# Gated DeltaNet: another order of the input products in the first two stretches, and other slots for the recurrences and inversions

## The chip, the cores and the metric

The kernel runs on one core of a Trainium2 chip. The metric is the device time of one execution, in microseconds (us). The engines of the core are PE (matrix products; its weight loads are counted apart as PEld), DVE (vector arithmetic), ACT (scalar functions and copies), POOL (a second, slower vector engine) and SP, which only issues DMAs here.

## The reference, cut to what matters

One inference step of a two-layer decoder trunk runs over 1104 tokens: a prompt of 1024, 16 meta tokens ahead of it and 64 tokens of eight sampled sequences. Layer 0 is a Gated DeltaNet with 8 key heads and 16 value heads of 128; layer 1 is an RWKV-7 layer that the change does not touch. Of layer 0:

```python
qkv, z, b, a = split(xn @ w_in)                 # 1024 -> 2*1024 + 2048 + 2048 + 32
qkv = silu(causal_conv(qkv, width 4))
q, k = l2norm(q), l2norm(k);  beta = sigmoid(b);  g = -exp(a_log) * softplus(a + dt_bias)
# per value head, chunk by chunk:
A = eye + strict_lower((k*beta) @ k.T * decay)
u, wk = solve(A, [v*beta, k*beta*exp(gc)])      # unit lower triangular
attn = lower(q @ k.T * decay)
v_new = u - wk @ S
o = (q*exp(gc)) @ S + attn @ v_new
S = S*exp(g_last) + k_dec.T @ v_new             # the recurrence over chunks
out = rmsnorm(o) * silu(z) @ w_out
```

The triangular solve needs the inverse of A for each chunk of 128 tokens, and S is carried from chunk to chunk.

## The kernel before

Layer 0 runs over eight **pairs** j = 0 to 7, one key head and its two value heads each. The input projection is done feature tile by feature tile of 128: keys k, queries q, the values v and w of the two heads, and the gates z and z' of the two heads (products x and y in the changed kernel). Each such product goes over three token segments of 384, 384 and 336, and each segment in two halves of 12 matmuls (an fp32 product as sums over high and low parts, `xc`, `xa`, `whi`, `wlo`). A half is called a **slot** here; a product is six slots. `products` in `layer0` yields them: 24 slots for k q v w of pair 0, numbered -24 to -1, and then 36 in each **stretch**: k of pair j, z z' of pair j-1, q, v, w of pair j. The last 12 are the gates of pair 7.

All the other work of the layer hangs on these slots. `gdn_events` fills a table of functions by a slot number, a fraction allowed, with `at(u, f)`; ahead of each slot, `before(u)` runs the functions that are due. PE and ACT then work in exactly the order in which the program writes their instructions. DVE, POOL and SP do not: a scheduler with its own idea of how long things take orders their instructions at compile time. What it chose is read from the order of the instructions. Each engine then works through its own list in order, and an instruction that waits holds up all behind it.

`front_events(j, ...)` prepares pair j, once its keys are there:
- decays, exponentials and the scores of k with k for the three segments (events `ed`, `ee`, `es`), which give A;
- the inversion of the diagonal 32x32 blocks of A, all 72 of them side by side (`inverse32`). It has 31 steps, and each is two DVE instructions: a product into `invtmp` (L570) and a subtraction from `invT` (L572), of growing and then shrinking shapes, from 72x31 to 72x256 and back to 72x31. The events `inv` issue them, two steps at a time (three for pair 0);
- `spread` (event `sp`): what is left of the steps, a turned copy (L740), the write of both to DRAM (g_t L743, g_u L742), and the reads back in another layout into `T1n` (L746) and `TT` (L753), all issued on SP;
- four merges, which build the inverse of 128 from blocks of 32: y32, u32, y64, u64, at 6.5, 4.5, 3.5 and 1.5 before a. y32 is the first that reads `T1n`; on PE it writes `rY`, and its DVE copies are L764;
- loads and products of the eight samples' states.

`chain_events(j, ..., a)` is the recurrence of pair j, from slot a = `first[j]` on: nine groups of tokens, each over three slots, for both heads. On DVE a group has X (L880, value rows less what the state gives), S (L902, the new state) and o (L913, the output); on PE these are the `rA` products. In group n, X comes at a + 3n - 1, S and o at a + 3n + 1. The recurrence of pair j-1 is thus running while the blocks of pair j are inverted, and DVE does both, with the conv taps (`cvy`, L523, four to a segment), the value rows (`vt`, `bv`) and the gate rows (`zg`).

Of the kernel before, what the change touches and what calls it, by code (L numbers as in the profile page):

```python
# [22 lines left out]
NEG = -1.0e30  # L23
ZF = 1
QF = 0


class Ctx:
# [7 lines left out]
class Builder:  # L36
# [883 lines left out]
    def gdn_events(self, G, open_, gate, swap):  # L920

        self.events = {}
        base = [36 * (j - 1) for j in range(9)]
        first = [9, 43] + [base[j + 1] + 6 for j in range(2, 8)]
        for u in (-22.9, -19.4, -16.8, -16.7, -16.6):
            self.at(u, gate)
        self.at(-13, swap)
        for j in range(8):
            self.chain_events(j, G, first[j])
            if j:  # L930
                self.front_events(j, G, base[j], base[j] + 18, first[j], open_, base[j] + max(0.3, first[j - 1] - base[j] - 3.4))
            else:
                self.front_events(0, G, -24, -18, first[0], None, None)

    def at(self, u, f, *a):
        self.events.setdefault(u, []).append(lambda: f(*a))
# [55 lines left out]
            for h in (0, 1):  # L992
                at((14.5, 23.5, 30.5)[s] + h, lambda s=s, h=h: self.gdn_norm_out(j, G[j], s, h))

    def front_events(self, j, G, b, qb, a, open_, e):

        g, at = lambda: G[j], self.at
        Sb = {}

        def states(h, q):  # L1000
            Sb[h, q] = self.sample_states(j, h, q)

        def read(h):
            self.gdn_sample_read(g(), h, [Sb[h, q] for q in (0, 1)])
        va = qb + 6
        at(b + 0.1, lambda: self.gdn_prep(j, g()))
        if j:
            at(b - 5.7, open_, j)
            at(b - 1.4, lambda: self.history_turn(g().H))
            k = max(b + 5.5, e + 4.7)  # L1010
            ed, ee, es = [e + 2 * s for s in range(3)], [k + 2 * s - 1.8 for s in range(3)], [k + 2 * s for s in range(3)]
            inv, per, kk, ss, rd = [k + 9.3 + n for n in range(15)], 2, (b + 11.8, qb + 4.2), b + 13.2, (qb + 6.4, qb + 9.9)
            sp = a - 9.9
        else:
            ed, ee, es = [-18.5, -18.4, -18.3], [-16, -15.2, -14.4], [-15.2, -14.4, -13.6]
            inv, per, kk, ss, rd = [-11.5 + n for n in range(10)], 3, (-12.2, -12.1), -12.8, (-7.6, -4.1)
            sp = -1
        for s in range(3):
            at(ed[s], lambda s=s: g().decay(s))
            for tt in range(3):  # L1020
                at(ee[s] + (0.7 if j else 0.25) * tt, lambda s=s, tt=tt: g().exps(s, tt))
            at(es[s], lambda s=s: g().scores(s))
            at(qb + (7.6, 16.4, 20.4)[s], lambda s=s: self.gdn_query_norms(g(), s))
        at(es[2] + 0.4, lambda: g().scales())
        at(es[2] + 0.7, lambda: g().blocks())
        for u in inv:
            at(u, lambda: g().steps(per))
        at(sp, lambda: g().spread())
        for n, u in enumerate((-6.5, -4.5, -3.5, -1.5)):
            at(a + u, lambda n=n: g().merges[n]())  # L1030
        at(kk[0], lambda: self.gdn_sample_keys(g(), 0))
        at(kk[1], lambda: self.gdn_sample_keys(g(), 1))
        for h, q in ((0, 0), (0, 1), (1, 0)):
            at(ss, states, h, q)
        at(rd[0], read, 0)
        at(rd[0] + 0.1, states, 1, 1)
        at(rd[1], read, 1)
        for h in (0, 1):
            for s in range(3):
                at(va + 6 * h + 5.4 + 2 * s, lambda h=h, s=s: self.gdn_value_rows(g(), h, s))  # L1040
        at(va + 12.95, lambda: self.last_tokens(j, g().H))

    def gdn_norm(self, j, G, s, os, ssq):

# [1077 lines left out]
    def layer0(self, top, right, xa, xc):  # L2122
# [20 lines left out]
        kh, kl = [h[:, k] for h in hi for k in range(4)], [l[:, k] for h in lo for l in h for k in range(l.shape[1])]  # L2143
# [3 lines left out]
        G = [None] * 8  # L2147
# [11 lines left out]
        self.gdn_events(G, open_, lambda: next(gate, None), swap)  # L2159

        def products():
            yield from G[0].keys(0)
            yield from self.gdn_queries(0, G[0], kh, kl, 2048)
            yield from self.gdn_values(0, G[0], 0, kh, kl, 2176)
            yield from self.gdn_values(0, G[0], 1, kh, kl, 1152)
            for j in range(1, 8):
                k = 128 * (j + 1)
                z = [4096 + 256 * (j - 1), 4224 + 256 * (j - 1)]
                va = 2048 + 256 * j
                yield from G[j].keys(z[0])  # L2170
                yield from self.gdn_gate(j - 1, G[j - 1], 0, kh, kl, z[1])
                yield from self.gdn_gate(j - 1, G[j - 1], 1, kh, kl, 128 * j)
                yield from self.gdn_queries(j, G[j], kh, kl, va)
                yield from self.gdn_values(j, G[j], 0, kh, kl, va + 128)
                yield from self.gdn_values(j, G[j], 1, kh, kl, 1024 + k if j < 7 else 4096 + 256 * 7)
            yield from self.gdn_gate(7, G[7], 0, kh, kl, 4224 + 256 * 7)
            yield from self.gdn_gate(7, G[7], 1, kh, kl)

        def before(u):
            while True:  # L2180
# [6 lines left out]
        with tc.manual_schedule(engines={mybir.EngineType.PE, mybir.EngineType.Activation}):  # L2187
            self.slot = -24
            for _ in products():
                before(self.slot + 1)  # L2190
                self.slot += 1
# [6 lines left out]
        sp = pool("stage", stage, side="right")  # L2198
# [343 lines left out]
```

## Time and profile before

| what | us |
|---|---|
| median of three runs | 2201.82 |
| lowest and highest | 2195.72, 2205.32 |
| the profiled execution | 2193.46 |
| its span, first to last instruction | 2191.7 |
| PE busy | 2051.0 (94%) |
| DVE busy | 1588.0 (72%) |
| ACT busy | 1291.8 (59%) |
| stretch 1, slots 0 to 35 | 141.9 |
| stretch 2 | 136.1 |
| stretch 3 | 119.2 |
| stretch 4 | 119.5 |

All times in the trace count from the start of the span. The shares of the whole span are means over two layers and many stretches; what the change does is read from the stretches. A row of a timeline is: start, duration, engine, line, operation, output and inputs, shapes, count, and in brackets the idle time of the engine ahead of it and what ended that. A row of waits is: the engine and line that waited, what it waited for, sum, times, longest. A row of windows is: from and to, length, then for each engine its busy time and, in brackets, its instructions, and at the end the granted PE clock (1.00 is full speed), the busy share of the DMA engines and GB/s. A row of groups is: line, engine, operation, names, shapes, count, busy time in us and mean of one in ns, and the idle time ahead of them.

### The profile page before, as it was taken

The page shows a single profiled execution, that of the slowest core. Times are in us where ns is not written, and L with a number is a line of the kernel's source. Part 1 is how long each engine was busy: PE and PEld are TensorE (multiplying, and loading weights), DVE is VectorE, ACT ScalarE, POOL GpSimd, SP SyncE. Part 2 cuts the span into 40 slices and gives each one's busy share as a digit, 9 for nine tenths or more (in the row PEclk, how much of TensorE's full clock was granted, in tenths as well). Part 3 has the DMA queues.
Part 4 walks back from the last instruction along what each step waited for, and adds up shares of the span by engine and source line. Part 5 has one row for each costly group of instructions (what it writes and reads, how often), then busy time and mean ns, then how long its engine had stood idle before and what let it go on. Part 6 is the DMA issues. An engine that isn't in the chain of part 4 may idle for free. (4 is left out here: it accounts for less than half of the span.)

```text
span 2191.7 us, 54812 instructions
## 1 busy us (share of the span) xinstructions
PE 2051.0 (94%) x20404; PEld 1908.7 (87%) x20404; DVE 1588.0 (72%) x4221; ACT 1291.8 (59%) x3761; POOL 844.7 (39%) x1125
## 2 busy tenths in 40 slices
PE   6869899999999999999899999889999999999997
PEld 5859799899999999999899999889888988888876
DVE  7967869788887979695334676757969657767755
ACT  5526466656566565656633365664847446777774
POOL 3423333334333333334231362344534344444444
PEclk9979999999999999999999999899999999999998
DMA  4423342333333433335345215655555376677764
GB/s 118 119 58 90 86 111 78 102 90 97 104 105 97 112 83 103 110 98 145 121 125 128 67 53 190 211 168 173 171 168 163 115 222 174 180 229 226 234 178 136
DMA packets 430661, 292.64 MB, mean 134 GB/s; under 512 B 147146, under 2 KB 412987, under 8 KB 430395
## 3 DMA queue, kind: packets, MB, share of 16 engines
q1 hardware_dynamic: 430394, 289.14, 45.9%
q8 instruction: 161, 2.64, 0.5%
q14 instruction: 106, 0.86, 0.1%
HBM read 197.68 MB, written 91.37 MB: 132 GB/s over the span
## 5 line engine op out<-in xcount | busy, mean ns | idle before, releaser
L90 POOL TENSOR_TENSOR wlo<-wraw,whi 128x512 fp32r<-128x512 f32 (+1 forms) x246 | 330.6, 1346 | 469.5 <-ACT whi L86 434.9
L76 PE MATMUL d<-xc,whi 128*128 128x384 f32 (+2 forms) x1006 | 279.7, 336 | 4.6 <-ACT whi L86 3.9
L523 DVE SCALAR_TENSOR_TENSOR cvy<-raw,cw,cvy 128x408 f32<-128x408 f32 (+2 forms) x288 | 192.5, 669 | 20.3 <-ACT cvy L62 18.8
L86 ACT CAST whi<-wraw 128x512 fp32r<-128x512 f32 (+1 forms) x246 | 149.7, 611 | 86.4 <-PE d L76 48.8
L76 PEld LDWEIGHTS d<-xc,whi 128*128 128x128 f32 (+1 forms) x1006 | 183.2, 189 | 7.4 <-ACT whi L86 4.6
L76 PE MATMUL d<-xc,wlo 128*128 128x384 f32 (+3 forms) x476 | 157.4, 339 | 2.6 <-POOL wlo L90 2.6
L76 PE MATMUL dz<-xc,whi 128*128 128x384 f32 (+1 forms) x480 | 153.7, 338 | 0.0
L76 PE MATMUL dv<-xc,whi 128*128 128x384 f32 (+1 forms) x480 | 152.2, 337 | 0.0
L76 PE MATMUL d<-xa,whi 128*128 128x384 f32 (+3 forms) x450 | 143.2, 342 | 1.6 <-DVE xb L1160 1.2
L62 ACT ACTIVATE o<-rA,gcol 128x128 f32<-128x128 f32 x128 | 42.1, 366 | 117.6 <-DVE S L902 117.3
L570 DVE TENSOR_TENSOR invtmp<-invA,invT 72x31 f32<-72x31 f32 (+15 forms) x248 | 102.5, 413 | 3.2
L76 PE MATMUL dv<-xa,whi 128*128 128x384 f32 (+1 forms) x288 | 99.0, 344 | 0.0
L572 DVE TENSOR_TENSOR invT<-invT,invtmp 72x31 f32<-72x31 f32 (+15 forms) x248 | 96.1, 388 | 3.3
L76 PE MATMUL dz<-xa,whi 128*128 128x384 f32 (+1 forms) x288 | 98.5, 342 | 0.0
L76 PEld LDWEIGHTS d<-xc,wlo 128*128 128x128 f32 (+1 forms) x476 | 89.2, 189 | 6.3 <-POOL wlo L90 3.5
L76 PEld LDWEIGHTS dz<-xc,whi 128*128 128x128 f32 x480 | 89.3, 188 | 4.6 <-issue 4.6
L76 PEld LDWEIGHTS dv<-xc,whi 128*128 128x128 f32 x480 | 89.1, 188 | 1.4 <-issue 1.4
L76 PEld LDWEIGHTS d<-xa,whi 128*128 128x128 f32 (+1 forms) x450 | 85.2, 192 | 4.8 <-issue 3.3
L76 PE MATMUL d<-xa,wlo 128*128 128x384 f32 (+3 forms) x252 | 85.6, 340 | 1.4 <-POOL wlo L90 1.4
L76 PE MATMUL dq<-xc,whi 128*128 128x384 f32 (+1 forms) x240 | 78.0, 342 | 3.0 <-ACT whi L86 3.0
L76 PE MATMUL dk<-xc,whi 128*128 128x384 f32 (+1 forms) x240 | 78.6, 347 | 0.0
L62 ACT ACTIVATE mixs<-xb,omu 128x64 f32<-128x64 f32 (+3 forms) x128 | 61.6, 521 | 18.3 <-DVE xc L90 8.6
(523 smaller groups left out, 6829.5 us busy)
## 6 DMA issues: line engine op xcount, KB each, us to landing
wraw<-in_gdn_w_in SPq DMA_DIRECT2D x96, 256.0 KB
wraw<-in_rwkv_w_rkvz SPq DMA_DIRECT2D x80, 256.0 KB
Sb<-in_state_gdn SPq DMA_DIRECT2D x64, 256.0 KB
sldcak<-cakd SPq DMA_DIRECT2D x24, 576.0 KB
wraw<-in_rwkv_w_o SPq DMA_DIRECT2D x42, 256.0 KB
E<-drow SPq DMA_DIRECT2D x24, 384.0 KB
attn<-drow SPq DMA_DIRECT2D x24, 384.0 KB
wraw<-in_gdn_w_out SPq DMA_DIRECT2D x36, 256.0 KB
```

Of the source, the lines that this page charges most:

```text
L62: return self.nc.scalar.activation(out, in_, func, bias=bias, scale=scale, **kw)
L76: self.nc.tensor.matmul(out, lhsT, rhs, start=start, stop=stop)
L86: nc.scalar.copy(hi, x)
L90: e.tensor_tensor(lo, x, hi.bitcast(F32), op=ALU.subtract)
L523: nc.vector.scalar_tensor_tensor(y[0][:, 0:wd], raw[:, k:k + wd], cw[k], y[0][:, 0:wd], op0=ALU.mult, op1=ALU.add)
L570: nc.vector.tensor_tensor(tmp, A[:, j, j + 1:32].unsqueeze(2).broadcast_to([nb, n, m]), Tv[:, j, 0:m].unsqueeze(1).broadcast_to([nb, n, m] ...
L572: nc.vector.tensor_tensor(Tv[:, j + 1:32, 0:m], Tv[:, j + 1:32, 0:m], tmp, op=ALU.subtract)
```

## The change

The order of the products stands in a table, `ORDER`, one string for each stretch. Stretch 1 has the gates of pair 0 first, then k v q w; stretch 2 has v ahead of q; stretch 3 on are as before. The slots `first`, at which the recurrences start, go from 9, 43, 78, 114 to 11, 47, 80, 114 for pairs 0 to 3, so that a merge of the same pair moves with them; pairs 4 to 7 keep theirs. The times of the other events are tied to the slot of the product that they need and to the start `a0` of the recurrence of the pair before. With k later in stretch 1, pair 1's scores start 7.2 slots later; its inversion events go from 19.6 to 33.6 to 26.2 to 38.1, its spread from 33.1 to 39.25. Pair 2's scores are 4 slots later, its spread 1.95. The inversion events of all pairs but 0 come every 0.85 slots instead of every slot, and for pairs 4 to 7 their spread is 3 slots earlier, and the loads of the samples' states 3.9 slots earlier. What is computed, and each instruction's kind and shape, stay as they are.

```diff
+ORDER = ("kqvw", "xykvqw", "kxyvqw", "kxyqvw", "kxyqvw", "kxyqvw", "kxyqvw", "kxyqvwXY")
...
-        first = [9, 43] + [base[j + 1] + 6 for j in range(2, 8)]
+        first = [11, 47, 80, 114] + [base[j + 1] + 6 for j in range(4, 8)]
...
-            if j:
-                self.front_events(j, G, base[j], base[j] + 18, first[j], open_, base[j] + max(0.3, first[j - 1] - base[j] - 3.4))
-            else:
-                self.front_events(0, G, -24, -18, first[0], None, None)
+            self.front_events(j, G, base[j] if j else -24, first[j], first[j - 1] if j else None, open_)
...
-    def front_events(self, j, G, b, qb, a, open_, e):
+    def front_events(self, j, G, b, a, a0, open_):
...
-        va = qb + 6
+        kb, qb, va, vb = (b + 6 * ORDER[j].index(c) for c in "kqvw")
...
-            k = max(b + 5.5, e + 4.7)
+            e = max(kb + 0.3, a0 - 3.4)
+            k = max(kb + 5.5, e + 4.7)
...
-            inv, per, kk, ss, rd = [k + 9.3 + n for n in range(15)], 2, (b + 11.8, qb + 4.2), b + 13.2, (qb + 6.4, qb + 9.9)
-            sp = a - 9.9
+            inv, per = [k + 8.7 + 0.85 * n for n in range(15)], 2
+            sp = max(k + 9 + 15 * 0.85, a0 + 17.2)
+            ss = max(kb + 6, a0 + 3.3)
+            kk = max(kb + 5.3, b + 11.8), qb + 4.2
+            u = max(qb + 6.4, a0 + 9.5)
+            rd = u, u + 3.5
...
-        for h in (0, 1):
-            for s in range(3):
-                at(va + 6 * h + 5.4 + 2 * s, lambda h=h, s=s: self.gdn_value_rows(g(), h, s))
-        at(va + 12.95, lambda: self.last_tokens(j, g().H))
+        for s in range(3):
+            for h, v in ((0, va), (1, vb)):
+                u = max(v + 5.4 + 2 * s, a0 + 9 * s + 5.8 + 0.2 * h if j else -99)
+                at(u, lambda h=h, s=s: self.gdn_value_rows(g(), h, s))
+        at(vb + 6.95, lambda: self.last_tokens(j, g().H))
```

`products` now walks through `ORDER` and calls the same functions as before, each with the weights of the product that follows it.

Three places show how the instructions move. A number behind a name is a tile's count in its program, and differs between the two kernels. The first place is PE around y32 of pair 0 (`rY`), at the start of stretch 1; `dk` and `dz` are halves of a key and a gate product. Before:

```order
L76 MATMUL dk_1479<-xa_103,whi_1267 128x384
L76 MATMUL dk_1479<-xa_103,wlo_1268 128x384
L76 MATMUL dk_1479<-xc_107,whi_1267 128x384
L73 MATMUL fss_1496<-ident_74,Q_1014 128x128 x3
L76 MATMUL rY_1504<-T1n_513,E_666 32x32 x12
L76 MATMUL rY_1505<-T1n_513,E_678 32x32 x12
L76 MATMUL rY_1506<-T1n_513,E_686 32x32 x12
L76 MATMUL dk_1479<-xc_107,whi_1332 128x384
```

and now:

```order
L77 MATMUL dz_1513<-xa_103,whi_1267 128x336
L77 MATMUL dz_1513<-xa_103,wlo_1268 128x336
L77 MATMUL dz_1513<-xc_107,whi_1267 128x336
L77 MATMUL rY_1530<-T1n_513,E_666 32x32 x12
L77 MATMUL rY_1531<-T1n_513,E_678 32x32 x12
L77 MATMUL rY_1532<-T1n_513,E_686 32x32 x12
L77 MATMUL dz_1513<-xc_107,whi_1332 128x336
```

The merge stood in the second segment of a key product and stands now in the third of a gate product, two slots on.

The second place is DVE where the inversion of pair 1 begins (the first `invtmp` row of 72x31), with the recurrence of pair 0 around it. Before:

```order
L880 SCALAR_TENSOR_TENSOR X_2236<-rA_2240,gcol_123,bv_1209 128x128
L880 SCALAR_TENSOR_TENSOR X_2237<-rA_2241,gcol_123,bv_1209 128x128
L1047 SCALAR_TENSOR_TENSOR ovar_2257<-ssq_1818,qeps_1005 128x6
L110 TENSOR_TENSOR on_t_2260<-ors_2259 128x6
L111 SCALAR_TENSOR_TENSOR on_t_2260<-on_t_2260,ovar_2257 128x6
L112 SCALAR_TENSOR_TENSOR ors_2259<-on_t_2260,ors_2259 128x6
L902 SCALAR_TENSOR_TENSOR S_1817<-S_1817,eglb_124,rA_2240 128x128
L902 SCALAR_TENSOR_TENSOR S_1817<-S_1817,eglb_124,rA_2241 128x128
L570 TENSOR_TENSOR invtmp_2328<-invA_2175,invT_2177 72x31
L572 TENSOR_TENSOR invT_2177<-invT_2177,invtmp_2328 72x31
L913 TENSOR_TENSOR o_2235<-o_2235,rA_2240 128x128
```

and now:

```order
L903 SCALAR_TENSOR_TENSOR S_1801<-S_1801,eglb_124,rA_2387 128x128
L524 SCALAR_TENSOR_TENSOR cvy_2441<-raw_2358,cw_393,cvy_2441 128x336
L914 TENSOR_TENSOR o_2381<-o_2381,rA_2386 128x128
L914 TENSOR_TENSOR o_2381<-o_2381,rA_2387 128x128
L524 SCALAR_TENSOR_TENSOR cvy_2441<-raw_2358,cw_393,cvy_2441 128x336
L881 SCALAR_TENSOR_TENSOR X_2500<-rA_2504,gcol_123,bv_1209 128x128
L881 SCALAR_TENSOR_TENSOR X_2501<-rA_2505,gcol_123,bv_1209 128x128
L571 TENSOR_TENSOR invtmp_2557<-invA_2396,invT_2398 72x31
L1069 SCALAR_TENSOR_TENSOR zg_1444<-mog_2522,hgn_402,zg_1444 128x384
L573 TENSOR_TENSOR invT_2398<-invT_2398,invtmp_2557 72x31
```

The first step stood behind S of group 3 of pair 0; it stands now behind X of group 5.

The third place is DVE where the inversion of pair 5 begins, in a later stretch. Before:

```order
L880 SCALAR_TENSOR_TENSOR X_9078<-rA_9082,gcol_123,bv_8116 128x128
L831 SCALAR_TENSOR_TENSOR zg_9122<-zg_9122,dz_9062 128x384
L110 TENSOR_TENSOR on_t_9105<-ors_9104 128x6
L111 SCALAR_TENSOR_TENSOR on_t_9105<-on_t_9105,ovar_9102 128x6
L112 SCALAR_TENSOR_TENSOR ors_9104<-on_t_9105,ors_9104 128x6
L902 SCALAR_TENSOR_TENSOR S_8651<-S_8651,eglb_124,rA_9081 128x128
L902 SCALAR_TENSOR_TENSOR S_8651<-S_8651,eglb_124,rA_9082 128x128
L570 TENSOR_TENSOR invtmp_9165<-invA_8993,invT_8995 72x31
```

and now:

```order
L881 SCALAR_TENSOR_TENSOR X_9078<-rA_9082,gcol_123,bv_8139 128x128
L571 TENSOR_TENSOR invtmp_9129<-invA_8999,invT_9001 72x31
L573 TENSOR_TENSOR invT_9001<-invT_9001,invtmp_9129 72x31
L571 TENSOR_TENSOR invtmp_9132<-invA_8999,invT_9001 72x60
L573 TENSOR_TENSOR invT_9001<-invT_9001,invtmp_9132 72x30x2
L832 SCALAR_TENSOR_TENSOR zg_9122<-zg_9122,dz_9062 128x384
```

Two steps of the inversion stand now ahead of S of group 3, where none stood. The inversions of pairs 2 to 4 begin, as before, behind S of group 3 of the pair ahead of them.

More of the change, by code (lines that the diff above doesn't have):

```diff
@@ L2161, in products @@
         def products():
[L2162 to L2177, printed above, removed]
+            todo = []
+            for j in range(8):
+                for c in ORDER[j]:
+                    if c == "k":
+                        todo.append((1024 + 128 * j, lambda w, j=j: G[j].keys(w)))
+                    elif c == "q":
+                        todo.append((128 * j, lambda w, j=j: self.gdn_queries(j, G[j], kh, kl, w)))
+                    elif c in "vw":
+                        h = "vw".index(c)
+                        todo.append((2048 + 128 * (2 * j + h), lambda w, j=j, h=h: self.gdn_values(j, G[j], h, kh, kl, w)))
+                    else:
+                        h = "xyXY".index(c)
+                        i, h = j - 1 + h // 2, h % 2
+                        todo.append((4096 + 128 * (2 * i + h), lambda w, i=i, h=h: self.gdn_gate(i, G[i], h, kh, kl, w)))
+            for n, (_, f) in enumerate(todo):
+                yield from f(todo[n + 1][0] if n + 1 < len(todo) else None)
         def before(u):
```

## The prediction

> **What bounds the kernel now.** I read the eight stretches of layer 0 first, because only they are touched, as windows of 36 product slots: length, then busy time of PE, PEld, DVE, ACT, POOL, and behind them the granted clock and the DMA share.
>
> ```profile
> 113.40:255.30 141.90, 119.14 (x1018) 113.32 (x1016) 108.50 (x308) 70.78 (x229) 42.46 (x65) 0.92 0.30 79
> 255.30:391.40 136.10, 121.12 (x1094) 115.41 (x1092) 104.72 (x300) 78.47 (x263) 50.88 (x73) 0.95 0.36 95
> 391.40:510.60 119.20, 117.98 (x1023) 112.59 (x1021) 96.05 (x276) 70.70 (x233) 41.94 (x63) 0.99 0.35 97
> 510.60:630.10 119.50, 117.43 (x1025) 111.08 (x1021) 101.24 (x280) 74.36 (x246) 44.08 (x66) 1.00 0.36 99
> ```
>
> From the third stretch on PE is busy 98 to 99% of the time, 119.2 / 36 = 3.31 us a slot. The first stretch loses 22.8 us and the second 15.0 us beside PE's work. The waits of PE over layer 0 (sum, times, longest) say where:
>
> ```profile
> PE rY L76 <- DMA T1n<-g_t: 32.7, 6, 20.1
> PE rA L76 <- DVE o L913: 5.5, 10, 0.9
> PE rA L76 <- DVE S L902: 3.2, 7, 0.9
> PE mog L73 <- ACT o L62: 2.8, 5, 0.6
> ```
>
> The big one is the first merge (rY, called y32) of a pair, which waits for the inverted blocks to come back through DRAM. PE's timeline shows it for pairs 0 to 3, and SP's the write g_t that opens the trip:
>
> ```profile
> 141.83 0.31 PE L76 MATMUL rY<-T1n,E 32*32 32x32 f32 x2 [20.10 <-DMA T1n<-g_t]
> 266.23 0.31 PE L76 MATMUL rY<-T1n,E 32*32 32x32 f32 x2 [8.61 <-DMA T1n<-g_t]
> 388.52 0.28 PE L76 MATMUL rY<-T1n,E 32*32 32x32 f32 x2 [2.51 <-DMA T1n<-g_t]
> 509.33 1.33 PE L76 MATMUL rY<-T1n,E 32*32 32x32 f32 x72
> ...
> 136.54 0.27 SPq L743 DMA_DIRECT2D g_t<-invT  x1
> 260.20 0.31 SPq L743 DMA_DIRECT2D g_t<-invT  x1
> 383.17 0.31 SPq L743 DMA_DIRECT2D g_t<-invT  x1
> 502.34 0.30 SPq L743 DMA_DIRECT2D g_t<-invT  x1
> ```
>
> The trip takes 5.3, 6.0 and 5.3 us for pairs 0 to 2. Pair 3 does not wait; at 5.3 us its blocks would be there at 507.6, 1.7 us early. What comes before g_t is the inversion, 31 steps of two instructions on DVE. From its first step to g_t, DVE is (window length, busy time):
>
> ```profile
> 202.90:260.20 57.30, 55.49 (x153) 1.00 0.25 73
> 329.00:383.20 54.20, 50.03 (x142) 1.00 0.26 77
> 451.00:502.30 51.30, 47.12 (x137) 1.00 0.26 77
> 571.10:621.80 50.70, 48.07 (x137) 1.00 0.26 78
> ```
>
> 92 to 97% busy: while it inverts, DVE is the bound, and the inversion cannot be paced more slowly or faster by its due slots, only by how many other instructions lie between its steps. And the first step starts where DVE's order lets it:
>
> ```profile
> 202.42 0.60 DVE L902 SCALAR_TENSOR_TENSOR S<-S,eglb,rA 128x128 f32<-128x128 f32 x2 [1.13 <-PE rA L76]
> 202.94 0.18 DVE L570 TENSOR_TENSOR invtmp<-invA,invT 72x31 f32<-72x31 f32 x1
> ...
> 329.02 0.18 DVE L570 TENSOR_TENSOR invtmp<-invA,invT 72x31 f32<-72x31 f32 x1
> ...
> 451.05 0.18 DVE L570 TENSOR_TENSOR invtmp<-invA,invT 72x31 f32<-72x31 f32 x1
> ```
>
> It stands right behind the S update of the other pair's group 3, which waits for PE. So up to y32 of pair 3 the program is one loop that never closes early: y32 of pair j, PE's slots up to the recurrence row that holds back the next inversion (61.1, 62.8, 62.5 us), DVE's inversion (57.3, 54.2, 51.3), the trip (6.0, 5.3, and 7.0 with its slack), y32 of pair j+1. The end of that loop moves everything behind it.
>
> **The change through this loop.** Total work is the same; the costs lie in where the rows stand.
>
> *Pair 0's wait.* y32 of pair 0 moves from event 2.5 to 4.5, so PE does two more slots first, and DVE's tail of the inversion has 13 conv taps in it instead of 16, against 2 gate rows more. A tap costs 0.675 us, a gate row 0.603 (groups of DVE in the pair-1 inversion; busy time, mean ns):
>
> ```profile
> L523 DVE SCALAR_TENSOR_TENSOR cvy<-raw,cw,cvy 128x408 f32<-128x408 f32 (+2 forms) x25 | 16.9, 675 | 1.1 <-ACT cvy L62 1.1
> L902 DVE SCALAR_TENSOR_TENSOR S<-S,eglb,rA 128x128 f32<-128x128 f32 x11 | 3.5, 338 | 0.0
> L913 DVE TENSOR_TENSOR o<-o,rA 128x128 f32<-128x128 f32 x12 | 3.2, 276 | 0.0
> L880 DVE SCALAR_TENSOR_TENSOR X<-rA,gcol,bv 128x128 f32<-128x128 f32 x10 | 3.2, 339 | 0.0
> L570 DVE TENSOR_TENSOR invtmp<-invA,invT 72x31 f32<-72x31 f32 (+15 forms) x31 | 12.6, 406 | 0.3
> L529 DVE SCALAR_TENSOR_TENSOR vt<-raw,cvy 128x64 f32<-128x64 f32 (+3 forms) x7 | 2.8, 427 | 0.0
> L1065 DVE SCALAR_TENSOR_TENSOR zg<-mog,hgn,zg 128x384 f32<-128x384 f32 x4 | 2.4, 603 | 0.0
> L822 DVE TENSOR_TENSOR bv<-f,sk 128x384 f32<-128x384 f32 x4 | 2.2, 548 | 0.0
> ```
>
> 3 x 0.675 - 2 x 0.603 = 0.8 us; I take 0.5, since one gate row is of the shorter form: the blocks come at 141.3 instead of 141.8. PE's wait shrinks by some 5 us, two slots without a recurrence, but these slots are work brought forward: what counts is that the loop starts 0.5 us earlier.
>
> *Leg to pair 1's inversion.* Before, its first step stands behind S of group 3, event 9 + 10 = 19. Now DVE's order has it behind X of group 5, event 11 + 14 = 25. From y32 that is 16.5 slots before and 20.5 now: 4 slots more on PE, at 3.31 us = 13.2. Bounds: a bare product half, without recurrence rows, is 12 matmuls at the 0.18 us from start to start below, 2.2 us, so 8.6 for four; above, stretch 1 took 141.9 / 36 = 3.94 with its waits, 15.8. I take 3.31, because a recurrence runs in these slots and PE has no long wait there.
>
> ```profile
> 273.35 0.33 PE L76 MATMUL dk<-xa,whi 128*128 128x384 f32 x1
> 273.53 0.33 PE L76 MATMUL dk<-xa,wlo 128*128 128x384 f32 x1
> ```
>
> First step: 141.3 + 61.1 + 13.2 = 215.6, against 202.9.
>
> *Pair 1's inversion.* Its steps now have fewer rows between them, counted in DVE's order: 4 X, 2 S, 4 o, 2 taps, 2 value rows and an attention row fewer; two key rows, one bv and four small rows more. 4 x 0.339 + 2 x 0.338 + 4 x 0.276 + 2 x 0.675 + 2 x 0.427 = 5.3 go, and 2.2 come (a key row as a value row, a small one at about 0.2): some 3.0 less, 54.3. The attention row, with the two times 384 elements of two gate rows, would take up to 1.2 more off; I leave it out for what the added rows may cost more. g_t at 269.9, y32 at 275.9 with the 6.0 us trip: **9.7 later than 266.2**. PE is there long before: it has 15.5 slots from event 25 to 40.5, 51 us, against 54.3 + 6.0. So the wait at pair 1 does not go, it stays at about 9 us.
>
> *Pair 2.* Events 53 and 36.5 become 57 and 40.5, the leg stays 16.5 slots: 62.8 us, first step at 338.7. Between its steps 2 X, 1 tap, 3 value rows and one bv more, 2 S and 2 o fewer: 0.68 + 0.68 + 1.28 + 0.55 - 0.68 - 0.55 = 2.0 more, 56.2. g_t 394.9, y32 at 400.2, **11.7 later**.
>
> *Pair 3.* Events 88 and 71.5 become 90 and 73.5: the leg again 62.5, first step 462.7. But y32 of pair 3 stays at 107.5, so the steps and the trip now have 17.5 slots instead of 19.5. Two taps, one value row and one bv more, 2 o and 1 gate row fewer: 1.35 + 0.43 + 0.55 - 0.55 - 0.60 = 1.2 more, 52.5. g_t 515.2, blocks at 520.5: **11.2 later than 509.3**, with PE 17.5 x 3.31 = 57.9 behind the first step, the blocks 57.8; the 1.7 us of slack are gone and the shift of the loop is passed on whole to all that follows.
>
> *Clock.* Behind a long wait PE is slow for a while (PE busy, then the granted clock):
>
> ```profile
> 266.20:268.00 1.80, 1.33 (x40) 0.50 0.43 65
> 268.00:270.00 2.00, 2.00 (x44) 0.50 0.29 44
> 270.00:272.00 2.00, 2.00 (x9) 0.57 0.24 37
> 272.00:274.00 2.00, 2.00 (x14) 1.00 0.28 46
> ...
> 386.00:388.50 2.50, 0.01 (x1) 0.86 0.68 137
> ...
> 391.00:393.00 2.00, 2.00 (x21) 0.50 0.29 46
> ```
>
> Some 5.2 us at half speed, 2.6 lost, also behind the 2.5 us wait of pair 2. Pairs 0 to 2 paid this before and pay it still, inside the legs that I carried over. Pair 3's y32 sits at the edge (57.9 against 57.8); if it waits by 2 us the same comes on top, if not nothing: I take the half, 1.3. The Trainium skill, TensorE: Matmul & The Clock Gate, Part 1, has the clock fall only after an idle window of about 3.4 us and come back after as long a busy one; here a 2.51 us wait was enough and the return took 5 us, so the measurement decides. By the page's figures a ramp would cost an estimated 1.7 us, and the sum would be lower by 0.5.
>
> *Steady stretches, pairs 5 to 7.* There the first two pairs of inversion rows now stand ahead of the S update of group 3 instead of behind it, and S of the next groups stands behind more of them. PE waits for S and o today 8.7 us in all, 17 times, about 1.1 a stretch. Four more such rows before S are 1.6 us at the 0.406 us of the first instruction's group, which PE may or may not have in hand: between 0 and 1.6 x 4 = 6.4, less the 2.8 of "mog", which may go as the heads' norms move: -2.8 to +6.4. I take +1.8, the middle. The earlier end of these inversions gives nothing, y32 does not wait there.
>
> *At no cost:* SP's queue moves no load ahead of g_t or the reads behind it in pairs 1 to 3 that was not there before; state loads of later pairs come some 4 slots sooner, into a DMA share of 0.36; weights follow the products' order.
>
> Sum: 11.2 + 1.3 + 1.8 = **14.3 us later**. The profiled execution took 2193.46 (span 2191.7); the three timed runs have a median of 2201.82, so it is the low end. Its differences are carried over: 2193.5 + 14.3 = 2207.8 on its own scale, 2201.8 + 14.3 = **2216** on that of the median.
>
> **Rivals.** *The loop shifts less.* With the four slots at 8.6 instead of 13.2 the shift is 11.2 - 4.6 = 6.6, no ramp at pair 3, nothing in the steady stretches: +4 to +9, 2206 to 2211. For it: several slots in that leg are gate products, which hang no conv taps on DVE. Against: the recurrence's rows are in every one of them.
>
> *The other side: pair 1's inversion ends on its due slots.* If the first step is not held back to X of group 5 in effect, because DVE runs well ahead of PE there and PE reaches event 25 early, or if the rows between the steps weigh 8 us less than I counted, g_t leaves before slot 39.5; then PE waits 2 to 3 us at pair 1 instead of 8.6 and nothing at pair 2, which with the 5 us of pair 0 gives 5 + 6 + 2.5 = 13.5 less, 2188. It decides at g_t of pair 1 by 260 us. For it: events and PE would allow it. Against: the quoted window is 97% busy, and 54 us of DVE rows do not fit the 14.5 slots (48 us) from event 25 to 39.5.
>
> *More is lost.* If S behind the inversion rows holds PE at every group of pairs 4 to 7, with 1.6 us at two of its groups in each of four stretches (13), and pair 3 ramps: 11.2 + 2.6 + 13 = 27, 2229.
>
> *The change does nothing of this* because DVE's order stays: excluded, its rows show the moves.
>
> **How the numbers follow.** What a measurement can tell from no change is about 0.5%, 11 us. My case (+11 and more) has 0.50, the larger loss 0.12, the smaller shift 0.28, the faster case 0.10. Slower therefore 0.62, same 0.28, faster 0.10. Likeliest 2216. Its own range is 2212 to 2222 (the leg's slots at 3.0 to 3.6 us, the ramp in or out, the steady term 0 to 4). For 8 in 10 I go down to 2198, which takes in the smaller shift and half of no change, and up to 2229.
>
> **What would show it.** DVE's first step of pair 1 near 215 us, g_t near 270, y32 of pairs 1, 2, 3 near 276, 400 and 520.5; PE's wait on T1n near 15 us for pair 0, 9 to 11 for pairs 1 and 2, small for pair 3. Stretches 4 to 7 at 119.5 to 120.5. The forecast is wrong if the first step of pair 1 comes by 208, or if the window from it to g_t is under 48 us; the steady term is wrong if a later stretch changes by more than 1.6 us.

## The result, and the profile after

The changed kernel takes 2223.55 us (median of four runs, 2222.2 to 2226.1), the kernel before beside it 2203.49 (2195.72 to 2205.32): a ratio of 1.012, 95% interval 1.0094 to 1.0146. Timed once more in a later comparison, again beside the kernel before, the ratio was 1.0132 (1.0108 to 1.0157). The first ratio is not that of its two medians, which lie 20.1 us apart, 0.9%; in the later comparison, with 17 runs of the kernel before, the medians lie 30.0 apart. By the ratio the change makes the kernel slower by 1.2%, some 26 us; 14 were forecast. The profiled execution took 2223.87 with a span of 2221.6, 29.9 more than the span before.

The stretches of 36 slots, as windows of the changed kernel (busy time of PE, PEld, DVE, ACT, POOL, then granted clock, DMA share, GB/s):

```profile
114.40:257.90 143.50, 120.19 (x1006) 113.57 (x1004) 101.85 (x289) 70.48 (x228) 43.07 (x68) 0.92 0.28 77
257.90:397.30 139.40, 120.25 (x1023) 114.89 (x1021) 104.33 (x300) 74.53 (x246) 47.37 (x66) 0.93 0.30 85
397.30:532.10 134.80, 123.74 (x1107) 117.63 (x1105) 105.59 (x298) 77.98 (x260) 44.99 (x70) 0.96 0.36 98
532.10:655.40 123.30, 119.19 (x1021) 113.10 (x1020) 96.00 (x276) 71.61 (x237) 42.84 (x63) 0.98 0.35 95
655.40:776.90 121.50, 117.56 (x1027) 111.23 (x1021) 98.89 (x280) 74.21 (x246) 44.29 (x66) 1.00 0.35 97
```

Every stretch is longer: 143.5, 139.4, 134.8, 123.3 and 121.5 us against 141.9, 136.1, 119.2, 119.5 and 118.9. The merge y32 of pair 2 stands two slots later and has passed from the second stretch into the third, so these two are best read together: 274.2 against 255.3. PE's timeline has the first merge of pairs 0 to 3, SP's the write that opens the trip, for pairs 1 to 3:

```profile
142.83 0.31 PE L77 MATMUL rY<-T1n,E 32*32 32x32 f32 x2 [16.22 <-DMA T1n<-g_t]
283.86 0.31 PE L77 MATMUL rY<-T1n,E 32*32 32x32 f32 x2 [13.49 <-DMA T1n<-g_t]
406.57 0.66 PE L77 MATMUL rY<-T1n,E 32*32 32x32 f32 x4 [3.48 <-DMA T1n<-g_t]
528.85 0.22 PE L77 MATMUL rY<-T1n,E 32*32 32x32 f32 x2 [3.15 <-DMA T1n<-g_t]
...
278.67 0.28 SPq L744 DMA_DIRECT2D g_t<-invT  x1
399.45 0.30 SPq L744 DMA_DIRECT2D g_t<-invT  x1
522.29 0.34 SPq L744 DMA_DIRECT2D g_t<-invT  x1
```

The wait at pair 0 is 3.9 us shorter, at pair 1 4.9 longer, at pair 3 there is a new one. The loop from y32 to y32 comes 1.0, 17.6, 18.1 and 19.5 us later than before at pairs 0 to 3. The later pairs add to it: y32 of pair 7 is at 1020.0 against 985.9, 34.1 later. At the start of layer 0's last slot it is still 33.7 (1060.4 against 1026.7), and layer 1, which the change does not touch in the program, then takes 3.8 us less (1161.2 against 1165.0). So there are three things to explain: the 19.5 of the loop, the 14.6 of the later pairs, and a layer 1 that answers.

The windows on DVE from the first inversion step to g_t, for pairs 1, 2, 3, 4 and 5 (length, busy, clock, DMA share, GB/s):

```profile
219.10:278.70 59.60, 52.37 (x147) 0.93 0.24 71
346.30:399.40 53.10, 49.49 (x144) 0.97 0.24 69
470.90:522.30 51.40, 48.50 (x139) 1.00 0.24 70
593.80:643.50 49.70, 46.75 (x132) 1.00 0.24 69
712.90:765.20 52.30, 48.15 (x137) 1.00 0.24 70
```

In pair 1's window DVE has fewer rows and less busy time than before (52.4 against 55.5 us), but is idle for 7.2 us instead of 1.8. The waits of DVE in that window, with sum, times and longest, name the reasons for 5.9 of the 7.2; the kernel before has one wait there, 1.1 us for ACT:

```profile
DVE on_t L111 <- POOL ors L103: 2.6, 2, 1.4
DVE S L903 <- PE rA L77: 1.9, 1, 1.9
DVE X L878 <- PE rA L77: 1.4, 1, 1.4
```

And DVE's timeline at the first step of pair 5, in the later stretches, shows what the forecast had not seen:

```profile
709.25 0.35 DVE L881 SCALAR_TENSOR_TENSOR X<-rA,gcol,bv 128x128 f32<-128x128 f32 x1
712.90 0.19 DVE L571 TENSOR_TENSOR invtmp<-invA,invT 72x31 f32<-72x31 f32 x1 [3.30 <-DMA invA<-ltd]
...
714.70 0.60 DVE L903 SCALAR_TENSOR_TENSOR S<-S,eglb,rA 128x128 f32<-128x128 f32 x2
```

The first step stands ahead of S of group 3, and the matrix that it reads is not there yet. DVE stands still for 3.3 us with S, o and the value rows behind it. Pairs 6 and 7 have the same wait, 2.9 and 3.5 us; the first step of pair 4 waits for nothing.

### The profile page after: what moved, and what is told of

It reads as the page before. It is cut to its first block, busy times and chain, and to the rows that moved or that the text cites. A ratio compares the mean times of both kernels' runs of the same rounds, so it can differ in the third digit from the quotient of the medians.

```text
span 2221.6 us, 54834 instructions
## 1 busy us (share of the span) xinstructions
PE 2057.5 (93%) x20404; PEld 1913.7 (86%) x20404; DVE 1584.2 (71%) x4221; ACT 1290.2 (58%) x3761; POOL 839.5 (38%) x1125
## 5 line engine op out<-in xcount | busy, mean ns | idle before, releaser
L573 DVE TENSOR_TENSOR invT<-invT,invtmp 72x31 f32<-72x31 f32 (+15 forms) x248 | 89.1, 359 | 3.6
L1327 DVE SCALAR_TENSOR_TENSOR mixs<-xb,pcol,mixs 128x320 f32<-128x320 f32 (+2 forms) x96 | 70.1, 740 | 5.2 <-ACT mixs L63 4.9
```

The source lines that it names most:

```text
L573: nc.vector.tensor_tensor(Tv[:, j + 1:32, 0:m], Tv[:, j + 1:32, 0:m], tmp, op=ALU.subtract)
L1327: nc.vector.scalar_tensor_tensor(x[:, f:], xb[:, 8 + a + f:8 + b], mu, x[:, f:], op0=ALU.mult, op1=ALU.add)
```

## The experiments

Positions are read from the traces as in the prediction: the start of y32 of pairs 1 to 3 on PE, and the start of layer 0's last slot. Each kernel has its own kernel before beside it, and ratios go by that.

### The later pairs: which of the new rules costs

`late_old` puts the events of the inversions, the spread and the sample loads of pairs 4 to 7 back:

```diff
-            inv, per = [k + 8.7 + 0.85 * n for n in range(15)], 2
-            sp = max(k + 9 + 15 * 0.85, a0 + 17.2)
-            ss = max(kb + 6, a0 + 3.3)
+            late = j >= 4
+            inv, per = [k + (9.3 + n if late else 8.7 + 0.85 * n) for n in range(15)], 2
+            sp = a - 9.9 if late else max(k + 9 + 15 * 0.85, a0 + 17.2)
+            ss = b + 13.2 if late else max(kb + 6, a0 + 3.3)
```

> The changed kernel with the events of the inversion, the spread and the sample loads of pairs 4 to 7 put back to those of before; all else as changed. In DVE's order the first step of pairs 5 to 7 then stands behind S of group 3 again. Theory 'blocked queue' (the first step of pairs 5 to 7 stands ahead of S and holds DVE about 3 us for the load of invA): stretches 5 to 7 go back from 121.5, 121.5 and 122.9 to 119 each, stretch 4 stays near 122 for the ramp behind the wait at pair 3; in all 9 to 11 us under the changed kernel. Rival 'the loss is carried over from the loop of pairs 0 to 3' (late buffers or transfers): stretches 5 to 7 stay over 121, within 3 us of the changed kernel.

`start_only` moves only the inversion events of these pairs back, all by 0.6 slots, and keeps the pace and the other new rules:

```diff
-            inv, per = [k + 8.7 + 0.85 * n for n in range(15)], 2
+            inv, per = [k + (9.3 if j >= 4 else 8.7) + 0.85 * n for n in range(15)], 2
```

> The changed kernel with only the start of the inversion events of pairs 4 to 7 moved back by 0.6 slots (9.3 instead of 8.7 behind the scores); pace of 0.85, early spread and early sample loads stay. DVE's first step stands behind S of group 3 again. Theory 'blocked queue': as late_old, 8 to 11 us under the changed kernel, stretches 5 to 7 at 119 to 119.5. Rival 'pace and early spread' (steps closer together hold S and X of the later groups, and the earlier loads collide): stretches 5 to 7 stay at 121 or more, at most 3 us gained.

In the traces both say the same: stretches 5 to 7 go back to 119.1, 118.9 and 119.6 us in late_old and to 119.1, 119.2 and 119.4 in start_only, and layer 0's last slot starts at 1051.7 and 1049.3 instead of 1060.4. DVE's first step of pair 5 in start_only, from the second execution of that kernel below, stands behind S again and waits for nothing:

```profile
712.47 0.61 DVE L903 SCALAR_TENSOR_TENSOR S<-S,eglb,rA 128x128 f32<-128x128 f32 x2
713.00 0.18 DVE L571 TENSOR_TENSOR invtmp<-invA,invT 72x31 f32<-72x31 f32 x1
```

The pace of 0.85, the early spread and the early sample loads stayed in start_only, and with them it gained all that late_old gained. So the blocked queue, and the 0.6 slots that brought it about, carry the loss of stretches 5 to 7. In stretch 4 the same 0.6 slots take out 2.8 us too, though no first step waited there: PE's waits from y32 of pair 3 to that of pair 4, beside the ramp, were 3.9 us in the changed kernel and 1.9 in start_only, and which row made the difference was not tried.

The totals, though, did not follow: 1.0123 (1.0106 to 1.014) for late_old and 1.0117 (1.0095 to 1.0138) for start_only, where the expectation was some 10 us, 0.5%, less than the changed kernel. The changed kernel and start_only were therefore timed on one chip beside each other, as `after_again` and `start_again`.

> The changed kernel as it is, beside the next one on the same chip, since the trace of start_only and late_old had layer 0 shorter by 11 and 9 us than the changed kernel but their totals no clear gain. Both theories: 1.010 to 1.014 of before, layer 0 ends near 1060.

> start_only once more, with more rounds and beside the changed kernel on one chip. Theory 'layer 1 scatters' (its length differs by some us from run to run whatever the kernel): 6 to 11 us under after_again. Rival 'layer 1 gives it back' (a fixed reply of layer 1 to when layer 0 ends): within 3 us of after_again, layer 1 again over 1170 us in the trace.

2224.25 us (1.0132, 1.0108 to 1.0157) and 2223.26 (1.012, 1.0093 to 1.0146): no difference that could be measured. Layer 0 was 8.0 us shorter again. Windows over stretch 5 and over layer 1, of after_again and then of start_again (PE busy, clock, DMA share, GB/s):

```profile
654.80:776.30 121.50, 117.59 (x1029) 1.00 0.35 97
1058.70:2220.60 1161.90, 1096.69 (x12269) 0.98 0.55 164
```

```profile
653.30:772.40 119.10, 117.14 (x1028) 1.00 0.37 99
1050.70:2224.60 1173.90, 1101.58 (x12268) 0.98 0.55 163
```

Layer 1 took 12.0 us more, in both executions of start_only (1173.6, 1173.9) against both of the changed kernel (1161.2, 1161.9). It repeats, so the theory of a layer 1 that scatters by itself falls for this pair. Its size is less sure: both profiled executions of start_only were the longest of their runs, and if layer 0 gained 8.0 in all runs, the medians, 1.0 us apart, leave an estimated 7 for layer 1. A fixed answer to when layer 0 ends fails too: rules_only and rules_start below differ by the same 0.6 slots, and there layer 1 went the other way, from 1170.2 to 1163.7, in one profiled execution of each. What differs is the order that the scheduler gave to layer 1. Against the changed kernel, PE's order in start_only is the same but for some small `fL` rows, while ACT, DVE, POOL and SP have rows of layer 1 in other places: the state updates of its samples (`Sb`), casts of weights (`whi`) and mixes on ACT, weight loads on SP. Of PE's waits over layer 1, of after_again and then of start_again, these three grew most:

```profile
PE d L77 <- ACT whi L87: 1.7, 1, 1.7
PE fVT L74 <- DVE G L1750: 2.2, 2, 1.2
```

```profile
PE d L77 <- ACT whi L87: 5.8, 2, 4.1
PE fVT L74 <- DVE G L1750: 5.3, 5, 2.0
PE drsr L77 <- DVE Sb L1988: 2.5, 3, 1.5
```

Together 9.7 us more, two of the three on rows of the kinds that moved. Other waits grew less, and two shrank by 5.2 together (`d` on ACT's `ev`, and `fL`); in all PE stood 7.1 us longer and was busy 4.9 longer. That the moved rows are the cause was not tried: no kernel kept layer 1's order fixed.

### The loop: the place of k, the later recurrences

`k_first` puts only the products of stretch 1 back, with the recurrences as late as in the change:

```diff
-ORDER = ("kqvw", "xykvqw", "kxyvqw", "kxyqvw", ...)
+ORDER = ("kqvw", "kxyvqw", "kxyvqw", "kxyqvw", ...)
```

> The changed kernel with the product order of stretch 1 alone put back to k z z' v q w (k first), and the recurrences as late as in the change. DVE's first step of pair 1 then stands behind S of group 3, not X of group 5. Theory 'late keys' (the scores of pair 1 come later by more slots than y32 of pair 0, so the loop from y32 to y32 gets longer): first step of pair 1 near 204 us, y32 of pairs 1, 2, 3 near 267, 390 and 512 instead of 284, 407 and 529; 14 to 17 us under the changed kernel. Rival 'late recurrences' (first = 11, 47, 80 costs, wherever k stands): y32 of pair 3 stays over 522, at most 6 us gained.

y32 of pairs 1 to 3: 272.6, 396.5 and 518.7, and layer 0's last slot at 1050.4. That takes back 10.2 us of the 19.5 at pair 3, between the two numbers expected: the first step of pair 1 stood at 207.9 instead of 219.1, as the late keys ask (2215.58 us, 1.0105, 1.0072 to 1.0138), but y32 of pair 1 was now held by PE itself, which reaches it at event 40.5; the timeline has no wait there.

```profile
272.21 0.49 PE L74 MATMUL fss<-ident,Q 128*128 128x128 f32 x3
272.63 0.54 PE L77 MATMUL rY<-T1n,E 32*32 32x32 f32 x22
```

The head of the loop was late as well: y32 of pair 0 came at 146.0, 3.2 us later than in the changed kernel, since DVE has 104 instead of 97 rows from the first step of pair 0's inversion to its turned copy. So both causes are there, and the place of k weighs more than the 10.2 show.

`first_47` has the later recurrences of pairs 1 and 2 alone, in the product order of before (and with the new rules of `rules_start`, below):

```diff
-        first = [9, 43] + [base[j + 1] + 6 for j in range(2, 8)]
+        first = [9, 47, 80, 114] + [base[j + 1] + 6 for j in range(4, 8)]
```

> rules_start with the recurrences of pairs 1 and 2 started later as in the change (47 and 80 instead of 43 and 78), product order of before. Theory 'merges moved later inside a loop that waits on DVE': the waits at pairs 1 and 2 change, PE reaches y32 of pair 1 at event 40.5, some 5 to 8 us later than the 263 of rules_start, and keeps that up to pair 3: y32 of pair 3 at 511 to 516, layer 0 ends 7 to 12 us later than rules_start. Rival 'only the place of k costs': layer 0 ends within 3 us of rules_start.

y32 of pairs 1 to 3: 267.8 without a wait, 388.1 and 509.9, with waits of 4.8 and 3.6 us at pairs 2 and 3; rules_start has 263.4, 381.6 and 504.4. Layer 0's last slot starts 8.8 us later (1030.8 against 1022.0), within the 7 to 12 expected though y32 of pair 3 lies 1 us below its range. 2201.2 us, 1.0019 (1.0003 to 1.0036), against 0.997 (0.9955 to 0.9985) of rules_start.

`first_11` moves only pair 0, two slots:

```diff
-        first = [9, 43] + [base[j + 1] + 6 for j in range(2, 8)]
+        first = [11, 43] + [base[j + 1] + 6 for j in range(2, 8)]
```

> rules_start with the recurrence of pair 0, and with it the merges of pair 0, two slots later (first 11 instead of 9), nothing else. The wait at pair 0 shrinks by 5 us. Theory 'loop': the first step of pair 1 stays 61 to 63 us behind y32 of pair 0, so the wait at pair 1 grows by as much as PE came forward, and layer 0 ends within 2 us of rules_start. Rival 'work brought forward pays': layer 0 ends 4 to 6 us earlier.

The wait at pair 0 fell by 0.9 only, not 5. DVE's order has 104 rows instead of 97 from the first step of pair 0's inversion to its turned copy, and g_t comes at 140.4 instead of 136.5. y32 of pair 0, then 145.64 against 141.7, is late by these 3.9 us, and y32 of pair 1 by 4.9; rules_start's row is the last one:

```profile
145.64 0.31 PE L77 MATMUL rY<-T1n,E 32*32 32x32 f32 x2 [19.11 <-DMA T1n<-g_t]
268.33 0.31 PE L77 MATMUL rY<-T1n,E 32*32 32x32 f32 x2 [7.15 <-DMA T1n<-g_t]
```

```profile
263.41 0.31 PE L77 MATMUL rY<-T1n,E 32*32 32x32 f32 x2 [5.83 <-DMA T1n<-g_t]
```

Layer 0's last slot starts 5.5 us later (1027.5), 2190.93 us, 0.9985 (0.9972 to 0.9998). Neither expectation held: the loop passes on what comes in at its head, as the theory of the loop says, but the two slots brought new DVE rows into the inversion, and so a loss and no mere shift of the wait.

`q_first2` puts back the products of stretch 2 alone:

```diff
-ORDER = ("kqvw", "xykvqw", "kxyvqw", "kxyqvw", ...)
+ORDER = ("kqvw", "xykvqw", "kxyqvw", "kxyqvw", ...)
```

> The changed kernel with the product order of stretch 2 put back (q ahead of v). Theory: it does not touch the loop, 144 and 145 rows between first step and turn of pair 2: y32 of pair 3 and the end of layer 0 within 3 us of the changed kernel. Rival 'the order of stretch 2 matters for pair 2's inversion': 4 us or more either way.

y32 of pair 3 at 530.0 and the last slot at 1061.6, both 1.2 us from the changed kernel; 1.0128 (1.0096 to 1.0159). The order of v and q in stretch 2 does not matter here.

Counted from y32 of pair 0 to y32 of pair 3, so without the head, the loop takes 367.5 us before, 362.7 in rules_start, 368.2 in first_47, 372.7 in k_first and 386.0 in the changed kernel. The new rules, with their closer steps, take 4.8 off, the later recurrences of pairs 1 and 2 add 5.5, and the place of k in stretch 1 adds 13.4. The 4.4 between first_47 and k_first, which differ up to there in the slot of pair 0 and in the order of stretch 2, were not taken apart.

### Does DVE's row count set the loop?

`rows_less` leaves out two of the four conv taps of the queries and of the second values of pair 1, 12 DVE rows, and so computes other values there; most of the rows stood in the inversion of pair 1:

```diff
-            for k in range(1, 4):
+            for k in range(1, 2 if ft in (1, 19) else 4):
                 nc.vector.scalar_tensor_tensor(y[0][:, 0:wd], raw[:, k:k + wd], cw[k], ...)
```

> The changed kernel with two of the three DVE taps of the conv left out for the queries and the second values of pair 1: 12 DVE rows of about 0.6 us, 7 us, out of the inversion of pair 1; the rest of the work stays (the conv of these two products is computed with two of four taps). Theory 'DVE rows set the loop, and the loop sets the end': g_t of pair 1 5 to 7 us earlier, y32 of pairs 1, 2 and 3 each earlier by about as much, layer 0 ends 4 to 7 us earlier than the changed kernel. Rival 'the inversion of pair 1 waits for PE and POOL': g_t within 2 us, the end too.

The window of pair 1 fell from 59.6 to 52.1 us:

```profile
218.20:270.30 52.10, 44.04 (x128) 0.97 0.27 81
```

y32 of pairs 1 to 3 came at 275.6, 398.8 and 521.2, earlier by 8.3, 7.8 and 7.6 us, and layer 0's last slot at 1051.5, by 8.9. Some of this is the head, since y32 of pair 0 came 1.3 earlier; against after_again, where it came 0.5 earlier, they are 7.6, 7.4, 7.4 and 7.2. So what is taken from DVE in one inversion is taken from the end of layer 0 nearly whole, through two later waits. The total, 1.0135 (1.0113 to 1.0157), showed nothing of it: layer 1 took 1168.0.

### The new rules without the new order, and a faster kernel

`rules_only` has the product order and the recurrences of before, with the new rules for the other events:

```diff
-ORDER = ("kqvw", "xykvqw", "kxyvqw", "kxyqvw", ...)
+ORDER = ("kqvw", "kxyqvw", "kxyqvw", "kxyqvw", ...)
-        first = [11, 47, 80, 114] + [base[j + 1] + 6 for j in range(4, 8)]
+        first = [9, 43] + [base[j + 1] + 6 for j in range(2, 8)]
```

> The kernel before in product order and starts of the recurrences, with only the new rules for the other events (pace 0.85, earlier start, spread and sample loads). In DVE's order the first steps of pairs 1 to 4 stay behind S of group 3, those of pairs 5 to 7 go ahead of it. Theory: y32 of pairs 1 to 3 within 3 us of before (266, 389, 509), stretches 5 to 7 at 121.5 instead of 119, 7 to 10 us slower than before. Rival 'the loss needs the new order': within 3 us of before.

Stretches 5 to 7 were 121.0, 121.1 and 122.6, as the blocked queue asks. But y32 of pairs 1 to 3 came at 262.4, 380.6 and 503.1: earlier than before by 3.9, 7.9 and 6.2, where no more than 3 were expected. The closer steps pay in the loop and cost behind it; 2199.3 us, 1.0018 (1.0005 to 1.0032).

`rules_start` adds to rules_only the 0.6 slots of start_only for pairs 4 to 7:

```diff
-            inv, per = [k + 8.7 + 0.85 * n for n in range(15)], 2
+            inv, per = [k + (9.3 if j >= 4 else 8.7) + 0.85 * n for n in range(15)], 2
```

> rules_only with the inversions of pairs 4 to 7 started 0.6 slots later, as in start_only: product order and recurrences of before, the new pace and spread. Theory (the loop of pairs 0 to 3 gains from steps that stand closer, and the blocked queue of pairs 5 to 7 is gone): y32 of pairs 1 to 3 at 262, 381 and 503 as in rules_only, stretches 5 to 7 at 119, layer 0 ends 6 to 7 us before the kernel before; total 4 to 9 us faster than before. Rival (closer steps only move the waits): layer 0 ends within 2 us of before.

y32 at 263.4, 381.6 and 504.4, stretches 5 to 7 at 119.3, 118.9 and 119.2, the last slot at 1022.0 against 1026.7 before, 4.7 earlier where 6 to 7 were expected; 2187.14 us, 0.997 (0.9955 to 0.9985). `pace_07` sets the steps of pairs 1 to 3 closer still:

```diff
-            inv, per = [k + (9.3 if j >= 4 else 8.7) + 0.85 * n for n in range(15)], 2
+            inv, per = [k + (9.3 + 0.85 * n if j >= 4 else 8.7 + 0.7 * n) for n in range(15)], 2
-            sp = max(k + 9 + 15 * 0.85, a0 + 17.2)
+            sp = max(k + 9 + 15 * (0.85 if j >= 4 else 0.7), a0 + 17.2)
```

> rules_start with the steps of pairs 1 to 3 every 0.7 slots instead of 0.85, and their spread earlier to match; DVE's order then has 142, 130 and 125 rows from the first step to the turn instead of 146, 137 and 130. Theory 'rows between': g_t of pairs 1 and 2 about 2 us earlier, the wait of y32 of pair 1 shrinks from 6 to 4, 1 to 3 us faster than rules_start. Rival 'closer steps hold S and X': the waits of PE on S, X and o grow by more than 2 us and it is no faster.

2179.66 us, 0.9939 (0.9916 to 0.9962): faster than both kernels, and by more than the 1 to 3 us under rules_start that were expected. The windows of pairs 1 to 3 on DVE, of rules_start and then of pace_07:

```profile
203.30:256.40 53.10, 52.44 (x147) 1.00 0.26 78
326.10:376.20 50.10, 47.68 (x139) 1.00 0.25 75
443.70:493.60 49.90, 46.03 (x132) 1.00 0.23 68
```

```profile
202.70:253.10 50.40, 49.23 (x141) 1.00 0.25 72
321.80:367.70 45.90, 43.42 (x131) 1.00 0.25 74
436.30:482.70 46.40, 43.52 (x125) 1.00 0.24 69
```

and its wait at pair 1:

```profile
258.91 0.24 PE L77 MATMUL rY<-T1n,E 32*32 32x32 f32 x2 [1.54 <-DMA T1n<-g_t]
```

It is 5.8 in rules_start and 8.6 before. Layer 0's last slot starts at 1015.4, 11.2 us before that of the kernel before. Less than this, 5.9 us, shows in the spans of the profiled executions (2185.8 against 2191.7), as layer 1 took 1170.4 in that one; it was the longest of its six runs, and the ratio of 0.9939 says some 13.

## Why the prediction was right and wrong

The side was right and the mechanism of the loop too: the change moves y32 of pairs 1 to 3 later, and all behind them follows. The time came out inside the range, but the size of the loss was nearly twice the forecast. Two terms of the sum failed: the time for which DVE stands still in pair 1's inversion, which had been put at nothing, and that in the steady stretches. That the time still lies in the range is in part luck: the range was wide for the sake of other rivals, and layer 1, which the sum held fixed, gave back 3.8 us.

- **Pair 0's wait** (forecast: blocks 0.5 us earlier): y32 at 142.8, 1.0 later. g_t also came 1.1 later, 137.6 against 136.5, and stretch 1 began 1.0 later, so this lies ahead of the change's rows. Other traces with the same rows there, after_again, start_only, late_old, q_first2 and rows_less, have y32 at 141.5 to 142.4, so the head of the loop scatters by more than the forecast 0.5. From its first step to g_t the inversion took 38.8 to 38.9 us in all six and 38.4 before: 0.4 longer, not 0.5 shorter.
- **The leg to pair 1's inversion** (forecast 13.2 more): 15.2 more, 219.1 - 142.8 = 76.3. Within the bounds that were given, 8.6 to 15.8, and near their upper end.
- **Pair 1's inversion** (forecast 3.0 shorter, 54.3): 2.3 longer, 59.6. This is the step that failed in the loop. The prediction took DVE to be busy from the first step to the last, since it had been so at 97%, and summed rows. The rows did weigh less, 52.4 us. But with S and X of other groups and the norm rows in other places, DVE stood for 7.2 us, most of it behind rows that waited for PE and POOL. The waits show this; no run moved those rows alone. Of the 8.0 us that y32 of pair 1 was later than forecast (283.9 against 275.9), 5.3 are this, 2.0 the leg, 1.5 the head of the loop; the trip was 0.8 shorter than the 6.0 carried over.
- **Pairs 2 and 3** (forecast 2.0 and 1.2 longer inversions): 53.1 and 51.4, 1.1 shorter and 0.1 longer than before. The trips were longer instead, 7.1 and 6.6 against 5.3. For pair 2 the prediction denied that a new load would stand ahead of the reads; SP's timeline has one, of the decays (`attn<-drow`), between the two writes.

```profile
399.45 0.30 SPq L744 DMA_DIRECT2D g_t<-invT  x1
400.56 0.33 SPq L647 DMA_DIRECT2D attn<-drow  x1
401.40 0.32 SPq L743 DMA_DIRECT2D g_u<-invA  x1
402.34 1.71 SPq L747 DMA_DIRECT2D T1n<-g_t  x3
```

  The reads themselves are issued 2.9 us behind g_t, as before (383.17 to 386.06), so the load cost no time in the queue, and the longer trip lies in the transfer; whether the load slowed it was not tried. PE's wait at pair 2 was 3.5, not the 9 to 11 forecast: on the way PE had lost 5.0 us to three other rows that did not hold the loop. y32 of pair 3 was 19.5 later, 11.2 forecast; nearly all of that miss was there at pair 1.
- **Clock at pair 3** (forecast 1.3, half a ramp): the wait came, 3.15 us, and with it the whole ramp. PE, busy time and granted clock:

```profile
525.95:529.37 3.42, 0.22 (x2) 1.00 0.53 115
529.37:532.78 3.41, 2.75 (x72) 0.50 0.33 52
532.78:536.20 3.42, 3.42 (x13) 0.50 0.25 39
536.20:539.61 3.41, 3.41 (x90) 1.00 0.39 97
```

  PE was busy for 6.2 us at half speed, so 3.1 were lost. That fits the 3.1 us by which y32 of pair 4 follows y32 of pair 3 more slowly in start_only (122.6 against 119.5), where the later pairs are as before.
- **The steady stretches** (forecast 1.8, of -2.8 to 6.4): this is the other term that was mis-sized. y32 of pairs 5 to 7 follow each other by 121.4, 121.6 and 122.8 instead of 119.0, 118.8 and 119.2, 8.8 in all, and pair 4 adds 2.8 beside the ramp. The prediction saw the first step move ahead of S and priced the two DVE rows, 0.4 us each. It did not ask whether the row could start there: it waits for a DMA, and a waiting row costs its wait to all behind it. start_only, which puts these rows behind S again, takes 8.0 to 11.1 us out of layer 0, 2.2 to 2.8 of it at pair 4, whose first step had no such wait. By the forecast's own sign, a later stretch off by more than 1.6 us, the term is wrong: stretches 5 to 7 are off by 2.6, 2.6 and 3.7.
- **Layer 1** was taken as unchanged. It moved by -5.6 to +8.9 us from kernel to kernel against the 1165.0 before, by as much as most of the effects that were looked for.

The rivals: a smaller shift did not come, nor did pair 1's inversion end by its due slots. "More is lost", which had 0.12, came nearest in size, 27 us, with S held behind inversion rows as its place; its price was put on the rows themselves, and the trace has it in the wait for the load.

Half of what the forecast said of the pace needs mending as well. The due slots do pace the inversion, through the order: with 0.85 and 0.7 the scheduler leaves fewer other rows between the steps, and y32 of pair 1 went from 266.2 to 262.4 and 258.9.

## What to carry to other kernels

When rows change places on an engine that works through its list in order, ask first whether each moved row can start at its new place, and only then what it costs: where a 0.2 us row waited some 3 us for a load, each of three stretches was 2.6 to 3.7 us longer, and moving it back took that out. A wait that is filled by moving the merge behind it later is not gained if a loop of latencies starts at that merge; count from one merge to the next, all round, and the sum of rows on the engine that bounds it is only the lower end of its part. And when a scheduler orders a whole program, time the part that was changed by itself in the trace, since the rest may be ordered anew and answer with as many microseconds.

## What the runs showed of the hardware that was not expected

A wait of PE of 3.15 us cost about as much again behind it: the clock was still 1.00 while PE waited, fell to 0.50 only 0.5 us after work came back, at 529.37, and stayed there for 6.8 us (rows above). In this trace, in that of the kernel before and in those of start_only, k_first, first_47 and pace_07, the granted clock has two values, 1.00 and 0.50, and in each all its changes lie whole steps of 3.41 us apart. So at the 2.51 us wait before the change it fell within the wait, at 387.79, 0.7 us ahead of the work. The Trainium skill, TensorE: Matmul & The Clock Gate, Part 1, describes a window of about 3.4 us that runs freely and is not reset when a kernel starts; the steps agree with that. Full speed came back 5.5 to 7.7 us after work resumed, behind the seven waits at y32 of the two kernels.
